# The step from cross-attention into the MLP done by token tile, and four distances of small work moved

## The chip, the cores and the metric

The kernel runs on one core of a Trainium2 chip. The metric is the device time of one execution in microseconds (us), lower is better. The engines are named as the profile names them: PE (TensorE, matrix products; PEld is its weight load), ACT (ScalarE), DVE (VectorE), POOL (GpSimd) and SP (SyncE, which here only issues the loads of weights).

## What is computed

One block of a streaming encoder, on 256 tokens of 2048 channels, everything in float32. Only the tail of the second sub-layer and the head of the third matter to most of the change:

```python
h = rms_norm(x, mix_pre_norm)
y = hybrid_mixer(h, ...)                 # gated DeltaNet, pooling, gates, output product
x = x + rms_norm(y, mix_post_norm)
h = rms_norm(x, xa_pre_norm)
m = rms_norm(mem, mem_norm)
y = memory_cross_attention(h, m, ...)    # ends with o @ w_xo, 2048 x 2048
x = x + rms_norm(y, xa_post_norm)
h = rms_norm(x, ffn_pre_norm)
u = causal_dwconv(h @ w_up, ffn_conv_w) + ffn_conv_b    # w_up: 2048 x 11008
a, b = split(u, 2)
y = (silu(a) * b) @ w_down
x = x + rms_norm(y, ffn_post_norm)
```

## The kernel before

**Weights.** Every weight product is made of three: each float32 operand is split into a rounded high part and the low rest, and high x high, high x low and low x high are added in PSUM. A weight arrives in tiles of 1 MB (`wraw`, 128 x 2048, on SP's queue). `wsplit` (L149 to L155) halves each: ACT casts 1024 columns to the high part (L153, `whi`), DVE subtracts to the low part (L154, `wlo`). Both live in rings of three buffers.

**Two kinds of product.** `proj_tm` (L190 ff.) makes 512 output channels of both token tiles (128 tokens each), tokens on the partitions: three matmuls of 512 columns for each of 16 input pieces and each token tile (L197, L198, L199). With `tail=n` its last 2n pieces are taken token tile by token tile, and `mid` is called in between; until now only the last product of the kernel (`dn3`) uses that. `proj_cm` makes one block of 128 output channels for all 256 tokens, channels on the partitions (L179): 16 matmuls with the high weights over 512 columns (high and low part of the activations side by side) and 16 with the low weights over 256.

**Small work.** The gated DeltaNet, the norms and the like are Python generators in two lanes. `tick()`, called between runs of matmuls, lets each lane take one step; `yield` or `wait(n)` in a generator is a distance of one or n ticks. So the distances decide between which matmuls small work is recorded. A scheduler then orders what is recorded, except instructions given to `pin`, which stay in program order on their engine.

**The four places of small work.** `first_convs` (L655 ff.) squares the token-major input `xt` on ACT, one 2048-wide tile after the other. `gdn_rest` makes decay matrices: two `gap` products (L734), an Exp of each on ACT (L738), a mask on POOL (L739), then four `kq` products on PE (L747) into the same ring of four PSUM tiles; further down it has a `wait(3)` after the step called p5. `mem_norm` squares the memory tokens, waits two ticks and calls `row_factors` (L294 to L311): a reduction, POOL's scale and power (L271, L273), a diagonal matrix on DVE (L305) and the matmuls `Rp` with it (L307).

**The step into the MLP** (L1182 to L1200). `pn.block` (L380 ff.) squares each product of w_xo on ACT (L279) and multiplies it by the gain on DVE (L384). `pn.scales` makes the reciprocal roots on POOL (L396, L398). For each quarter q of the channels, `pn.piece` (L401 ff., DVE L403) normalises it and adds the residual for both token tiles, `transpose_in` (L240 to L260) turns it by matmuls against `ident` (L249) into two PSUM tiles of 256 channels and splits it into the tile `h3T` (ACT L256 for the high part, DVE L258 for the low part, both reading the PSUM tile), and `square_sum` squares it (ACT L279).

**The MLP's first half.** `up(blk)` (L1203 to L1215) makes a block by `proj_cm`, adds its two halves (`cm_sum`: ACT L185, DVE L186), multiplies by the row factor (L1208) and convolves (ACT L1209, DVE L1212). Blocks come in pairs `ua`, `ub`; after `ua` follows Silu (L1219, with an activation table to load), after `ub` the product of the two and its split `gT` (L1221, ACT L238, DVE L239).

Of the kernel before, what the change touches and what calls it, by code (L numbers as in the profile page):

```python
# [8 lines left out]
F32 = mybir.dt.float32  # L9
# [16 lines left out]
def kernel(  # L26
# [102 lines left out]
    def wait(n):  # L129
        for _ in range(n):  # L130
            yield
# [26 lines left out]
    def pin(ins, keep=True):  # L158
        if keep:
            tc.keep_in_program_order(ins)  # L160
# [73 lines left out]
    def getX(tiles):  # L234
        return lambda kt: tiles[kt // 4][:, kt % 4]
# [37 lines left out]
        nc.gpsimd.tensor_tensor(out=r, in0=r, in1=mhalf[:, 0:1], op=ALU.pow)  # L273
        return r

    def square_sum(src, dst, name):

        junk = tmp.tile([P, 512], F32, tag="j512", name=f"j_{name}")
        nc.scalar.activation(junk, src, AF.Square, accum_out=dst)  # L279

    def pre_norm(src, gi, name, tiles, ss):

# [82 lines left out]
    class PostNorm:  # L365
# [11 lines left out]
                         for t in range(NT)]  # L377
            self.r = []

        def block(self, ps, nb, ts=range(NT)):  # L380
            sl = slice(nb * 512, (nb + 1) * 512)
            for t in ts:
                square_sum(ps[t], self.ss[t][:, nb:nb + 1], f"{self.name}{nb}{t}")
                nc.vector.tensor_tensor(out=self.y[t][:, sl], in0=ps[t], in1=self.g[:, sl],  # L384
                                        op=ALU.mult)
# [15 lines left out]
        def piece(self, t, q):  # L401
            sl = slice(q * 512, (q + 1) * 512)
            nc.vector.scalar_tensor_tensor(  # L403
                out=self.y[t][:, sl], in0=self.y[t][:, sl], scalar=self.r[t][:, 0:1],
                in1=self.x[t][:, sl], op0=ALU.mult, op1=ALU.add)
            return self.y[t][:, sl]


# [203 lines left out]
    def gdn_group(gi):  # L612
# [33 lines left out]
        for hl in range(4):  # L646
# [3 lines left out]
            if h == 0:  # L650
                xps = [conv_in(ps, f"{c}{n}") for c, ps in zip("qkv", ps_first)]
                dec = decays(ps_first[3])
                next(dec)

                def first_convs(n=n, hl=hl, vc=vc):  # L655
                    ss0 = [sml.tile([P, 1], F32, tag="ss", name=f"s0_{t}", bufs=4)
                           for t in range(NT)]
                    yield from wait(1)
                    for t in range(NT):
                        pin(nc.scalar.activation(xt[t], xt[t], AF.Square, accum_out=ss0[t]))  # L660
                        yield
                    yield from wait(2)
                    R0.extend(row_factors(ss0, "h", True))
                    yield
                    for i, dst in enumerate((KQ[:, hl, :, 1, :], KQ[:, hl, :, 0, :], vc)):
                        conv_silu(xps[i], i, dst, f"{'qkv'[i]}{n}", R0[0])
                        yield
                        yield
                    lanes["a"].append(head_tok(n, hl, vc))
                    yield from wait(8)  # L670

                lanes["b"].append(first_convs())
                lanes["b"].append(dec)
                z_gate(raw_z)
                continue
# [17 lines left out]
    def gdn_rest(gi, g_, KQ, V, zs, ktok, ss):  # L693
# [30 lines left out]
        for b in range(2):  # L724
# [8 lines left out]
            for a in range(2):  # L733
# [327 lines left out]
    def mem_norm():  # L1061
        mcm = [b8(f"mcm{i}").rearrange("p (k s) -> p k s", k=8) for i in range(2)]
        for i in range(2):
            nc.gpsimd.dma_start(mcm[i], mem_cm[i])
        yield from wait(8)
        ss = yield from cm_squares(mcm, "me")
        yield from wait(2)
        R, _ = row_factors(ss, "me")
        yield from wait(2)
        yield from norm_cm(mcm, R, 2, "me", memT)  # L1070
# [106 lines left out]
            step(lanes["b"])  # L1177
    A = getX(aT)
    pn = PostNorm(1, lambda t: x1[t * P:(t + 1) * P, :], "xa")
    for nb in range(4):  # L1180
        pn.block(proj_tm(w_xo[nb], A, 16, f"xo{nb}"), nb)

    x2 = dram.tile([S, D], F32, name="x2")
    pn.scales()
    ss = new_ss("h3")
    h3T = []
    for q in range(4):
        ys = [pn.piece(t, q) for t in range(NT)]  # L1190
        d = xtile(f"h3T{q}")
        transpose_in(d, lambda t: ys[t], pre_sb[:, 3, 4 * q:4 * q + 4], f"h3{q}")
        h3T.append(d)
        for t in range(NT):
            square_sum(ys[t], ss[t][:, q:q + 1], f"h3{t}{q}")
    for t in range(NT):
        nc.gpsimd.dma_start(x2[t * P:(t + 1) * P, :], pn.y[t])
    H3 = getX(h3T)
# [122 lines left out]
```

## Time and profile before

| | |
|---|---|
| three runs | 2013.08, 2013.47, 2014.16 us; median 2013.47 us |
| profiled execution | 2014.26 us, its span 2012.5 us |
| granted clock of TensorE, mean | 0.998 |
| busy, share of the span | PE 99%, PEld 85%, DVE 67%, ACT 57%, POOL 6% |
| loaded and stored | 380 MB, 188 GB/s of HBM traffic over the span |

A span is the time from the first to the last instruction of the profiled execution; 1.8 us of the execution lie outside it. The busy share of PE in the page counts modelled ends of matmuls, so 99% does not mean that a matmul of full size was always in the array. The profile's clock is given as a share of full speed: 1.00 is 2.4 GHz, 0.50 is 1.2 GHz.

### The profile page before, as it was taken

To read this page: it belongs to the slowest core of one execution; us is meant where nothing else is said; L and a number is where in the kernel's file an instruction comes from. 1 tells how busy PE (TensorE), PEld (TensorE's weight loads), DVE (VectorE), ACT (ScalarE), POOL (GpSimd) and SP (SyncE) were. 2 spreads that over 40 slices of the span, in tenths; PEclk is the share of its full clock that TensorE was granted. 3 is DMA by queue.
4 is the path that set the end of the run, shared out by engine and by line. 5 is a ranking of instruction groups with operands and counts; after the bars stand their busy time and mean duration, and the time that the engine had idled before them with its cause. 6 is when DMAs were issued, how large, how long until landed. Compare 5 with 4: busy or idle time off the path is not lost.

```text
span 2012.5 us, 27745 instructions
## 1 busy us (share of the span) xinstructions
PE 1993.8 (99%) x10842; PEld 1708.6 (85%) x10842; DVE 1346.0 (67%) x2046; ACT 1138.0 (57%) x1902; POOL 112.2 (6%) x154
## 2 busy tenths in 40 slices
PE   9999999999999999999999999999999999999998
PEld 7888888888888888888888888788888888888886
DVE  6786776768746855767555554787777777754444
ACT  6777766767655544556454444665655555544443
POOL 0420211101100000000000000100000000000000
PEclk9999999999999999999999999999999999999999
DMA  8544454444445666556555555555555555565554
GB/s 309 186 159 156 168 169 145 168 168 165 165 153 195 225 229 210 183 191 212 189 189 186 188 175 200 207 192 188 189 188 189 189 189 188 191 240 192 195 192 142
DMA packets 57333, 379.97 MB, mean 189 GB/s; under 512 B 7024, under 2 KB 8304, under 8 KB 12656
## 3 DMA queue, kind: packets, MB, share of 16 engines
q1 hardware_dynamic: 54288, 361.41, 52.6%
q0 software_dynamic: 2192, 15.73, 2.1%
q8 instruction: 85, 1.39, 0.3%
q10 hardware_dynamic: 720, 1.05, 0.2%
q14 instruction: 48, 0.39, 0.1%
HBM read 371.87 MB, written 6.29 MB: 188 GB/s over the span
## 4 chain that ended last, share of the span: by engine, by line
PE 94%; ACT 2%; DMA 2%; issue 1%; POOL 1%; DVE 1%; SPq 0%; DVEq 0%; POOLq 0%; ACTq 0%
PE cm_ua L179 12%; PE cm_ub L179 12%; PE cm_xk L179 4%; PE cm_xq L179 4%; PE cm_kg L179 4%; PE tm_dn L198 4%; PE tm_dn L197 4%; PE tm_dn L199 4%; PE cm_qg L179 4%; PE cm_vg L179 4%; PE cm_p L179 2%; PE tm_ga L198 1%; PE tm_xv L197 1%; PE tm_ya L199 1%; PE tm_xv L198 1%; PE tm_ga L199 1%
## 5 line engine op out<-in xcount | busy, mean ns | idle before, releaser
L154 DVE TENSOR_TENSOR wlo_dn<-raw_dn,whi_dn 128x1024 fp32r<-128x1024 f32 (+1 forms) x88 | 105.5, 1200 | 117.5 <-ACT whi_dn L153 117.3
L179 PE MATMUL cm_ua<-h3T,whi_ua 128*128 128x512 f32 x688 | 166.6, 393 | 0.5 <-DVE h3T L258 0.5
L153 ACT CAST whi_dn<-raw_dn 128x1024 fp32r<-128x1024 f32 (+1 forms) x88 | 91.1, 1035 | 133.1 <-PE tm_dn L199 128.4
L179 PE MATMUL cm_ub<-h3T,whi_ub 128*128 128x512 f32 x688 | 165.9, 391 | 0.0
L179 PEld LDWEIGHTS cm_ua<-h3T,whi_ua 128*128 128x128 f32 x688 | 126.6, 189 | 25.7 <-DVE h3T L258 0.9
L179 PEld LDWEIGHTS cm_ub<-h3T,whi_ub 128*128 128x128 f32 x688 | 126.6, 188 | 24.7 <-ACT whi_ub L153 0.4
L197 PE MATMUL tm_dn<-whi_dn,gT 128*128 128x512 f32 x344 | 133.8, 389 | 0.0
L198 PE MATMUL tm_dn<-wlo_dn,gT 128*128 128x512 f32 x344 | 133.8, 389 | 0.0
L199 PE MATMUL tm_dn<-whi_dn,gT 128*128 128x512 f32 x344 | 133.8, 389 | 0.0
L153 ACT CAST whi_ua<-raw_ua 128x1024 fp32r<-128x1024 f32 x86 | 90.4, 1051 | 76.3 <-PE cm_ub L179 60.5
L153 ACT CAST whi_ub<-raw_ub 128x1024 fp32r<-128x1024 f32 x86 | 90.2, 1049 | 72.2 <-PE cm_ua L179 62.2
L154 DVE TENSOR_TENSOR wlo_ua<-raw_ua,whi_ua 128x1024 fp32r<-128x1024 f32 x86 | 104.8, 1219 | 7.6 <-ACT whi_ua L153 3.0
L154 DVE TENSOR_TENSOR wlo_ub<-raw_ub,whi_ub 128x1024 fp32r<-128x1024 f32 x86 | 104.7, 1218 | 0.5 <-PE cm_ua L179 0.5
L179 PEld LDWEIGHTS cm_ua<-h3T,wlo_ua 128*128 128x128 f32 x688 | 88.3, 191 | 3.4
L179 PEld LDWEIGHTS cm_ub<-h3T,wlo_ub 128*128 128x128 f32 x688 | 88.2, 191 | 3.4
L179 PE MATMUL cm_ua<-h3T,wlo_ua 128*128 128x256 f32 x688 | 89.5, 283 | 0.0
L179 PE MATMUL cm_ub<-h3T,wlo_ub 128*128 128x256 f32 x688 | 89.2, 283 | 0.0
L1212 DVE SCALAR_TENSOR_TENSOR ua_ub<-xp,fw_sb,ua_ub 128x256 f32<-128x256 f32 x86 | 41.7, 485 | 55.2 <-ACT ua_ub L1209 53.7
L197 PEld LDWEIGHTS tm_dn<-whi_dn,gT 128*128 128x128 f32 x344 | 64.6, 188 | 13.5
L199 PEld LDWEIGHTS tm_dn<-whi_dn,gT 128*128 128x128 f32 x344 | 64.6, 188 | 13.5
L198 PEld LDWEIGHTS tm_dn<-wlo_dn,gT 128*128 128x128 f32 x344 | 64.6, 188 | 13.2
L154 DVE TENSOR_TENSOR wlo_xv<-raw_xv,whi_xv 128x1024 fp32r<-128x1024 f32 x32 | 39.1, 1225 | 40.9 <-ACT whi_xv L153 38.8
(429 smaller groups left out, 5045.5 us busy)
## 6 DMA issues: line engine op xcount, KB each, us to landing
raw_ua<-in_w_up_dram SPq DMA_DIRECT2D x43, 1024.0 KB, 4.9
raw_ub<-in_w_up_dram SPq DMA_DIRECT2D x43, 1024.0 KB, 4.9
raw_dn<-in_w_dn_dram SPq DMA_DIRECT2D x40, 1024.0 KB, 4.8
raw_gb<-in_w_gb_dram SPq DMA_DIRECT2D x16, 1024.0 KB, 4.8
raw_ga<-in_w_ga_dram SPq DMA_DIRECT2D x16, 1024.0 KB, 4.9
raw_ya<-in_w_ya_dram SPq DMA_DIRECT2D x16, 1024.0 KB, 4.9
raw_mo<-in_w_mo_dram SPq DMA_DIRECT2D x16, 1024.0 KB, 4.8
raw_xk<-in_w_xk_dram SPq DMA_DIRECT2D x16, 1024.0 KB, 4.9
```

Source lines behind the costliest of these rows:

```text
L153: pin(nc.scalar.copy(hi[:, :m], raw[:, s:s + m]), keep)
L154: pin(nc.vector.tensor_tensor(out=lo[:, :m], in0=raw[:, s:s + m], in1=hi[:, :m].bitcast(F32), op=ALU.subtract), keep)
L179: pin(nc.tensor.matmul(ps[:, 0:S] if lo else ps, lhsT=w[:, (j0 + k) * P:(j0 + k + 1) * P], rhs=xk[:, 0, :] if lo else xk.rearrange("p a s ...
L197: nc.tensor.matmul(ps[t], lhsT=xh, rhs=wh, start=(k == 0), stop=False)
L198: nc.tensor.matmul(ps[t], lhsT=xh, rhs=wl, start=False, stop=False)
L199: nc.tensor.matmul(ps[t], lhsT=xl, rhs=wh, start=False, stop=(k == KT - 1))
L1212: nc.vector.scalar_tensor_tensor(out=a, in0=xp[:, 1 + j:1 + j + S], scalar=fw_sb[:, blk, j:j + 1], in1=a, op0=ALU.mult, op1=ALU.add)
```

## The change

It has two parts. First, the step into the MLP: the last product of w_xo is taken with `tail=3`, so that token tile 0 is finished 18 matmuls ahead of token tile 1, and its norm, its scale and three of its four pieces are recorded there. The weights of the first two up blocks (`w_up[0]`, `w_up[43]`) are loaded and split ahead of that product into four tiles of their own. These two blocks are then computed by (quarter q, token tile t): `h3_in` transposes four 128 x 128 squares into one PSUM tile, `h3_split` splits them one by one (four on ACT, four on DVE), `up_mm` makes the 16 matmuls of that quarter and tile for both blocks. All this, with the pieces and squares between, is pinned in the order written. The splits of the next two blocks' weights (`up_next`) are pinned as well, three of the four halves around the last two `up_mm`, the fourth where block `ub1` is recorded. The squares of token tile 1 follow them.

Second, four distances: the squares of `first_convs` are taken in halves and its waits are set anew, `gdn_rest` yields twice in place of once after its second gap and waits 4 in place of 3 after p5, and `mem_norm` waits 4 in place of 2.

```diff
     def first_convs(n=n, hl=hl, vc=vc):
-        ss0 = [sml.tile([P, 1], F32, tag="ss", name=f"s0_{t}", bufs=4)
-               for t in range(NT)]
-        yield from wait(1)
+        ss0 = [sml.tile([P, 2], F32, tag="ss0", name=f"s0_{t}") for t in range(NT)]
         for t in range(NT):
-            pin(nc.scalar.activation(xt[t], xt[t], AF.Square, accum_out=ss0[t]))
-            yield
-        yield from wait(2)
+            for s in range(2):
+                yield
+                v = xt[t][:, 1024 * s:1024 * s + 1024]
+                pin(nc.scalar.activation(v, v, AF.Square, accum_out=ss0[t][:, s:s + 1]))
+        yield
...
-        yield from wait(8)
+        yield from wait(7)
...
-            yield
+            yield from wait(1 + b)
...
-        yield from wait(3)
+        yield from wait(4)
         subs("t5", (Me, P5, LO5, 32, Te), (P5, Me, UP5, 32, Me))
...
-        yield from wait(2)
+        yield from wait(4)
         R, _ = row_factors(ss, "me")
...
-    for nb in range(4):
+    for nb in range(3):
         pn.block(proj_tm(w_xo[nb], A, 16, f"xo{nb}"), nb)
+    up_parts = []
+    for half in range(2):
+        raw = wp.tile([P, 2048], F32, tag="raw", name=f"raw_up{half}")
+        for i in range(2):
+            hl = b8(f"wup{half}{i}", F32R)
+            sl = slice(i * 1024, (i + 1) * 1024)
+            nc.sync.dma_start(raw[:, sl], w_up[KFF * i][:, half * 1024:(half + 1) * 1024])
+            split_to(hl[:, 0:1024], hl[:, 1024:2048], raw[:, sl])
+            up_parts.append((hl[:, 0:1024], hl[:, 1024:2048]))
+    def first_token_tile(ps):
+        pn.block([ps] * 2, 3, [0])
+        pn.scales([0])
+        for q in range(3):
+            pn.piece(0, q)
+    ps = proj_tm(w_xo[3], A, 16, "xo3", 3, first_token_tile)
...
-    pn.scales()
-    h3T = []
+    h3T = [xtile(f"h3T{q}") for q in range(4)]
+    ps_up = [ps_acc(f"cm_up{i}") for i in range(2)]
+    def h3_in(q, t):
+        tp[q, t] = ps_g(f"tp_h3{q}{t}")
+        for k in range(4):
+            c = (4 * q + k) * P
+            pin(nc.tensor.transpose(tp[q, t][:, k * P:(k + 1) * P], pn.y[t][:, c:c + P], ident))
+    def h3_split(q, t):
+        tsl = slice(t * P, (t + 1) * P)
+        for k in range(4):
+            gk = pre_sb[:, 3, 4 * q + k:4 * q + k + 1]
+            v = tp[q, t][:, k * P:(k + 1) * P]
+            pin(nc.scalar.activation(h3T[q][:, k, 0, tsl], v, AF.Identity, scale=gk))
+            pin(nc.vector.scalar_tensor_tensor(out=h3T[q][:, k, 1, tsl], in0=v, scalar=gk,
+                                               in1=h3T[q][:, k, 0, tsl].bitcast(F32),
+                                               op0=ALU.mult, op1=ALU.subtract))
+    def up_mm(q, t):
+        tsl = slice(t * P, (t + 1) * P)
+        for lo in (False, True):
+            for i in range(2):
+                w = up_parts[q // 2 * 2 + i][lo]
+                for k in range(4):
+                    j = (4 * (q % 2) + k) * P
+                    kt = 4 * q + k
+                    ps = ps_up[i].rearrange("p (a s) -> p a s", a=2)
+                    out = ps[:, 0, tsl] if lo else ps[:, :, tsl]
+                    rhs = H3(kt)[:, 0, tsl] if lo else H3(kt)[:, :, tsl]
+                    pin(nc.tensor.matmul(out, lhsT=w[:, j:j + P], rhs=rhs,
+                                         start=(not lo and kt == 0), stop=(lo and kt == 15)))
...
+    h3_in(0, 0)
+    h3_in(1, 0)
+    h3_split(0, 0)
+    pn.block(ps, 3, [1], True)
+    pn.scales([1])
+    h3_split(1, 0)
+    up_mm(0, 0)
+    h3_in(2, 0)
+    pn.piece(0, 3, True)
+    h3_split(2, 0)
+    up_mm(1, 0)
+    h3_in(3, 0)
+    h3_square(0, 0)
+    pn.piece(1, 0, True)
+    pn.piece(1, 1, True)
+    h3_split(3, 0)
+    up_mm(2, 0)
+    h3_in(0, 1)
+    h3_split(0, 1)
+    h3_square(0, 1)
+    up_mm(3, 0)
+    h3_in(1, 1)
+    pn.piece(1, 2, True)
+    h3_split(1, 1)
+    h3_square(0, 2)
+    up_mm(0, 1)
+    h3_in(2, 1)
+    pn.piece(1, 3, True)
+    h3_split(2, 1)
+    h3_square(0, 3)
+    up_mm(1, 1)
+    h3_in(3, 1)
+    h3_split(3, 1)
+    up_next = [wsplit(wraw(w_up[KFF * i + 1], 2048, f"up1{i}"), 2048, f"up1{i}", True)
+               for i in range(2)]
+    first_next = [next(up_next[0])]
+    up_mm(2, 1)
+    up_mm(3, 1)
+    first_next.append(next(up_next[0]))
+    first_next.append(next(up_next[1]))
     for q in range(4):
...
+        h3_square(1, q)
...
     def up(blk, name):
-        ps = proj_cm(w_up[blk], H3, name)
+        i = blk // KFF
+        if blk % KFF > 1:
+            ps = proj_cm(w_up[blk], H3, name)
+        elif blk == 1:
+            ps = proj_cm(None, H3, name, parts=first_next[:2])
+        elif blk % KFF:
+            ps = proj_cm(None, H3, name, parts=first_next[2:] + [next(up_next[1])])
+        else:
+            ps = ps_up[i]
```

Of `gdn_rest` the two waits are shown, the first after each gap (b is 0, then 1). Now the order in which instructions stand on an engine, at three places.

**PE, behind the last product of w_xo.** `tm_xo` is that product, `tp_h` are the transposes, `cm_ua` and `cm_ub` the first two up blocks. Before, from the tenth transpose behind it on:

```order
L249 MATMUL tp_h_0_11505<-ident,py_xa_10866 128x128
L249 MATMUL tp_h_1_11514<-ident,py_xa_10866 128x128
L249 MATMUL tp_h_1_11514<-ident,py_xa_10865 128x128
L249 MATMUL tp_h_1_11514<-ident,py_xa_10866 128x128
L179 MATMUL cm_ua_11609<-h3T_11479,whi_ua_0_11612 128x512
L179 MATMUL cm_ub_11661<-h3T_11479,whi_ub_0_11664 128x512
L249 MATMUL tp_h_0_11530<-ident,py_xa_10865 128x128
L179 MATMUL cm_ua_11609<-h3T_11479,whi_ua_0_11612 128x512 x2
L249 MATMUL tp_h_1_11539<-ident,py_xa_10865 128x128
L179 MATMUL cm_ua_11609<-h3T_11479,whi_ua_0_11612 128x512
L179 MATMUL cm_ua_11609<-h3T_11504,whi_ua_0_11612 128x512
```

With the change (`cm_up` are the same two blocks; 128x2x128 is a matmul of 256 columns):

```order
L199 MATMUL tm_xo_11349<-whi_xo_14_0_11448,aT_10851 128x512
L1215 MATMUL tp_h_11506<-ident,py_xa_10871 128x128 x4
L1215 MATMUL tp_h_11511<-ident,py_xa_10871 128x128 x4
L1239 MATMUL cm_up_11504<-h3T_11500,wup_11331 128x2x128 x4
L1239 MATMUL cm_up_11505<-h3T_11500,wup_11335 128x2x128 x4
L1239 MATMUL cm_up_11504<-h3T_11500,wup_11331 128x128 x4
L1239 MATMUL cm_up_11505<-h3T_11500,wup_11335 128x128 x4
L1215 MATMUL tp_h_11554<-ident,py_xa_10871 128x128 x4
L1239 MATMUL cm_up_11504<-h3T_11501,wup_11331 128x2x128 x4
```

The matmuls of the two blocks move between the transposes, in eight groups of 16, each of half the columns, and the whole of PE's work here is in written order.

**ACT, the splits of h3** (`j_xa` and `j_h` are squares; the semaphore in brackets is what the instruction waits for, DVE_49 counts DVE's work). Before:

```order
L256 ACTIVATE h3T_11479<-tp_h_0_11480,pre_sb 128x256 [waits PE_49]
L256 ACTIVATE h3T_11479<-tp_h_1_11489,pre_sb 128x256 [waits PE_49]
L279 ACTIVATE j_h_11523,nss_h_11475<-py_xa_10865 128x512 [waits DVE_49,Activation_49]
L256 ACTIVATE h3T_11479<-tp_h_0_11480,pre_sb 128x256 [waits DVE_49]
L256 ACTIVATE h3T_11479<-tp_h_1_11489,pre_sb 128x256 [waits DVE_49]
L256 ACTIVATE h3T_11504<-tp_h_0_11505,pre_sb 128x256 [waits PE_49]
L256 ACTIVATE h3T_11504<-tp_h_1_11514,pre_sb 128x256 [waits PE_49]
```

With the change:

```order
L279 ACTIVATE j_xa_11470,pss_xa_10875<-tm_xo_11348 128x512 [waits PE_49]
L1222 ACTIVATE h3T_11500<-tp_h_11506,pre_sb 128x128 [waits PE_49]
L1222 ACTIVATE h3T_11500<-tp_h_11506,pre_sb 128x128 [waits DVE_49] x3
L279 ACTIVATE j_xa_11524,pss_xa_10876<-tm_xo_11349 128x512
L1222 ACTIVATE h3T_11501<-tp_h_11511,pre_sb 128x128 [waits PE_49]
L1222 ACTIVATE h3T_11501<-tp_h_11511,pre_sb 128x128 [waits DVE_49] x3
L1222 ACTIVATE h3T_11502<-tp_h_11554,pre_sb 128x128 [waits PE_49]
L1222 ACTIVATE h3T_11502<-tp_h_11554,pre_sb 128x128 [waits DVE_49] x3
```

Reads of two PSUM tiles in turn become four reads of one tile, the last three of them each behind a wait for DVE.

**ACT, before the last half of block `ub1`** (`t_ua` is the sum of a finished `ua` block, L1318 and L1308 are now the lines of Silu and of the first convolution step). Before, `whi_ub_1024_11774` is that half:

```order
L185 COPY t_ua_11653<-cm_ua_11609 128x256 [waits PE_49]
L153 CAST whi_ub_0_11770<-raw_ub_11768 128x1024 [waits DVE_49,DMAHW6_49,PE_49,Activation_49]
L185 COPY t_ub_11705<-cm_ub_11661 128x256 [waits PE_49]
L1209 ACTIVATE ua_ua_11652<-xp_94,fb_sb,fw_sb 128x256 [waits DVE_49]
L153 CAST whi_ub_1024_11774<-raw_ub_11768 128x1024 [waits PE_49,Activation_49]
L153 CAST whi_ua_0_11824<-raw_ua_11822 128x1024 [waits DMAHW7_49,PE_49,Activation_49]
L1219 ACT_TABLE_LOAD
L1219 ACTIVATE ua_ua_11652<-ua_ua_11652 128x256 [waits DVE_49]
L1209 ACTIVATE ua_ub_11704<-xp_96,fb_sb,fw_sb 128x256
L185 COPY t_ua_11759<-cm_ua_11715 128x256 [waits PE_49]
```

With the change it is `whi_up_1024_11875`:

```order
L185 COPY t_ua_11814<-cm_up_11504 128x256 [waits PE_49]
L185 COPY t_ub_11823<-cm_up_11505 128x256 [waits PE_49]
L1308 ACTIVATE ua_ua_11813<-xp_94,fb_sb,fw_sb 128x256 [waits DVE_49]
L1308 ACTIVATE ua_ub_11822<-xp_96,fb_sb,fw_sb 128x256 [waits DVE_49]
L185 COPY t_ua_11867<-cm_ua_11833 128x256 [waits PE_49]
L1318 ACT_TABLE_LOAD
L1318 ACTIVATE ua_ua_11813<-ua_ua_11813 128x256 [waits DVE_49]
L1308 ACTIVATE ua_ua_11866<-xp_98,fb_sb,fw_sb 128x256 [waits DVE_49]
L238 CAST gT_11802<-ua_ub_11822 128x256 [waits DVE_49]
L1318 ACTIVATE ua_ua_11866<-ua_ua_11866 128x256 [waits DVE_49]
L153 CAST whi_up_1024_11875<-raw_up_11727 128x1024
```

The cast of that half moves from before the Silu of the first pair to behind the sum, the convolution and the Silu of the second `ua` block.

## Rows read from the trace of the kernel before

**Rows 1.** The page: chain that ended last, shares of the span by engine.

```profile
PE 94%; ACT 2%; DMA 2%; issue 1%; POOL 1%; DVE 1%; SPq 0%; DVEq 0%; POOLq 0%; ACTq 0%
```

**Rows 2.** What PE waited for: us in total, times, longest.

```profile
PE kq_g L747 <- ACT UD_g L738: 3.6, 4, 0.9
PE tp_h L249 <- DVE py_xa L403: 2.5, 3, 1.3
...
PE Rp_me L307 <- DVE dg_me L305: 0.6, 1, 0.6
```

**Rows 3.** Chain that ended last, 1276 to 1316: start us, us, what.

```profile
1281.36 0.24 PE tm_xo L199
...
1283.56 2.09 DVE py_xa L403 x3
...
1290.67 0.66 PE tp_h L249 x6
...
1304.01 4.43 PE cm_ua L179 x27
1308.44 5.57 PE cm_ub L179 x32
```

**Rows 4.** Windows: length; busy PE, PEld, DVE, ACT, POOL; PEclk, DMA share, GB/s.

```profile
1282.00:1283.00 1.00, 0.08 (x1) 0.11 (x2) 0.98 (x2) 1.00 (x3) 0.51 (x2) 1.00 0.88 139
...
1287.00:1288.00 1.00, 1.00 (x6) 0.66 (x4) 1.00 (x4) 1.00 (x4) 0.00 (x0) 0.50 0.00 0
```

**Rows 5.** Timeline, 926 to 931.5: ACT and DVE on transposed tiles; brackets: idle before, releaser.

```profile
928.40 0.83 ACT L256 ACTIVATE h2T<-tp_h,pre_sb 128x256 fp32r<-128x256 f32 x2
928.90 0.88 DVE L258 SCALAR_TENSOR_TENSOR h2T<-tp_h,pre_sb,h2T 128x256 fp32r<-128x256 f32 x2 [1.44 <-ACT h2T L256]
929.42 0.86 ACT L256 ACTIVATE h2T<-tp_h,pre_sb 128x256 fp32r<-128x256 f32 x2 [0.19 <-DVE h2T L258]
```

**Rows 6.** Lines L874 and L753: shortest, median, longest ns of one 128x128 from PSUM.

```profile
L874 ACT ACTIVATE TM_g<-X_g,br_g x32: 347/362/374, 181.2 to 592.9; 128x128 f32<-128x128 f32 x32
...
L753 DVE SCALAR_TENSOR_TENSOR UD_g<-kq_g,nbr_g,UD_g x32: 340/342/351, 122.8 to 518.0; 128x128 f32<-128x128 f32 x32
```

**Rows 7.** Timeline, 1288.4: one square of 512 columns on ACT.

```profile
1288.40 0.65 ACT L279 ACTIVATE j_h<-py_xa 128x512 f32<-128x512 f32 x1
```

**Rows 8.** Chain, 81 and 836 us: matmuls of 256 columns and of one.

```profile
81.20 1.91 PE cm_kg L179 x16
...
836.00 1.69 PE sq_me L332 x16
```

**Rows 9.** Chain, 839 us: POOL's power in the row factors.

```profile
839.42 0.58 POOL rstd_me L273
```

**Rows 10.** Timeline of ACT, 1308 to 1312: after a ua block.

```profile
1308.75 1.28 ACT L1219 ACT_TABLE_LOAD   x1
1310.04 0.42 ACT L1219 ACTIVATE ua_ua<-ua_ua 128x256 f32<-128x256 f32 x1
1310.37 0.59 ACT L1209 ACTIVATE ua_ub<-xp,fb_sb,fw_sb 128x256 f32<-128x256 f32 x1
1310.86 0.35 ACT L185 COPY t_ua<-cm_ua 128x256 f32<-128x256 f32 x1
1311.11 1.05 ACT L153 CAST whi_ua<-raw_ua 128x1024 fp32r<-128x1024 f32 x1
```

**Rows 11.** Timeline, 117 to 125: kq and the Exps.

```profile
119.32 1.89 PE L747 MATMUL kq_g<-KQ_g 128*128 128x256 f32 x8
...
121.44 1.09 ACT L738 ACTIVATE UD_g<-gap_g 128x512 f32<-128x512 f32 x2
...
122.09 1.99 PE L747 MATMUL kq_g<-KQ_g 128*128 128x256 f32 x8 [0.88 <-ACT UD_g L738]
```

**Rows 12.** Timeline of ACT at the start: the first cast of w_z.

```profile
34.33 2.00 ACT L153 CAST whi_zg<-raw_z 128x1024 fp32r<-128x1024 f32 x2 [1.36 <-DMA raw_z<-in_w_z_dram]
```

**Rows 13.** Groups of ACT: the casts for w_xo, idle before them, and what ended it.

```profile
L153 ACT CAST whi_xo<-raw_xo 128x1024 fp32r<-128x1024 f32 x32 | 33.7, 1054 | 44.0 <-PE tm_xo L199 40.6 <-PE tm_xv L199 3.3
```

More of the change, by code (lines that the diff above doesn't have):

```diff
@@ L274, in rstd_of, with square_sum @@
         return r
-    def square_sum(src, dst, name):
+    def square_sum(src, dst, name, keep=False):
         junk = tmp.tile([P, 512], F32, tag="j512", name=f"j_{name}")
-        nc.scalar.activation(junk, src, AF.Square, accum_out=dst)
+        pin(nc.scalar.activation(junk, src, AF.Square, accum_out=dst), keep)
     def pre_norm(src, gi, name, tiles, ss):
@@ L378, in __init__, with block @@
             self.r = []
-        def block(self, ps, nb, ts=range(NT)):
+        def block(self, ps, nb, ts=range(NT), keep=False):
             sl = slice(nb * 512, (nb + 1) * 512)
             for t in ts:
-                square_sum(ps[t], self.ss[t][:, nb:nb + 1], f"{self.name}{nb}{t}")
-                nc.vector.tensor_tensor(out=self.y[t][:, sl], in0=ps[t], in1=self.g[:, sl],
-                                        op=ALU.mult)
+                square_sum(ps[t], self.ss[t][:, nb:nb + 1], f"{self.name}{nb}{t}", keep)
+                pin(nc.vector.tensor_tensor(out=self.y[t][:, sl], in0=ps[t],
+                                            in1=self.g[:, sl], op=ALU.mult), keep)
             if nb == 2:
@@ L399, in scales, with piece @@
                 self.r.append(r)
-        def piece(self, t, q):
+        def piece(self, t, q, keep=False):
             sl = slice(q * 512, (q + 1) * 512)
-            nc.vector.scalar_tensor_tensor(
+            pin(nc.vector.scalar_tensor_tensor(
                 out=self.y[t][:, sl], in0=self.y[t][:, sl], scalar=self.r[t][:, 0:1],
-                in1=self.x[t][:, sl], op0=ALU.mult, op1=ALU.add)
+                in1=self.x[t][:, sl], op0=ALU.mult, op1=ALU.add), keep)
             return self.y[t][:, sl]
@@ L655, in first_convs @@
                 def first_convs(n=n, hl=hl, vc=vc):
-                    ss0 = [sml.tile([P, 1], F32, tag="ss", name=f"s0_{t}", bufs=4)
-                           for t in range(NT)]
-                    yield from wait(1)
+                    ss0 = [sml.tile([P, 2], F32, tag="ss0", name=f"s0_{t}") for t in range(NT)]
                     for t in range(NT):
-                        pin(nc.scalar.activation(xt[t], xt[t], AF.Square, accum_out=ss0[t]))
-                        yield
-                    yield from wait(2)
+                        for s in range(2):
+                            yield
+                            v = xt[t][:, 1024 * s:1024 * s + 1024]
+                            pin(nc.scalar.activation(v, v, AF.Square,
+                                                     accum_out=ss0[t][:, s:s + 1]))
+                    yield
                     R0.extend(row_factors(ss0, "h", True))
@@ L1185 @@
+    def first_token_tile(ps):
[4 more added lines that the diff above has]
+    ps = proj_tm(w_xo[3], A, 16, "xo3", 3, first_token_tile)
     x2 = dram.tile([S, D], F32, name="x2")
-    pn.scales()
     ss = new_ss("h3")
-    h3T = []
-    for q in range(4):
[L1190 to L1195, printed above, removed]
+    h3T = [xtile(f"h3T{q}") for q in range(4)]
@@ new lines @@
+    H3 = getX(h3T)
+    ps_up = [ps_acc(f"cm_up{i}") for i in range(2)]
+    tp = {}
+    def h3_in(q, t):
[12 more added lines that the diff above has]
+                                               op0=ALU.mult, op1=ALU.subtract))
@@ new lines, in h3_square @@
+    def h3_square(t, q):
+        square_sum(pn.y[t][:, q * 512:(q + 1) * 512], ss[t][:, q:q + 1], f"h3{t}{q}", True)
+    h3_in(0, 0)
[17 more added lines that the diff above has]
+    h3_split(0, 1)
@@ L1196 @@
+    first_next.append(next(up_next[1]))
+    for q in range(4):
+        h3_square(1, q)
     for t in range(NT):
         nc.gpsimd.dma_start(x2[t * P:(t + 1) * P, :], pn.y[t])
-    H3 = getX(h3T)
     R3, _ = row_factors(ss, "h3")
```

## The prediction

> **What bounds the kernel now.** First the shares of the chain that ended last: PE holds 94% of it [rows 1]. Time can only go where PE waits, so the second view is what PE waited for [rows 2]: four waits for the Exp behind the `kq` products (3.6 us together), three waits of the h3 transposes for the pieces (2.5 us), one of `Rp_me` (0.6 us). The change aims at these three. The third view is the chain around the step [rows 3]: the last matmul of w_xo starts at 1281.36 and is done at 1281.60, which I call E. The third up block (`ua1`) ends at 1308.44 = E+26.84, the fourth (`ub1`) at 1308.44 + 5.57 = 1314.01 = E+32.41. The first two blocks would have ended at E+21.27 had the third run at full speed (26.84 - 5.57). The fourth view, windows of 1 us [rows 4], shows the rest of the loss: PE is busy 0.08 in the microsecond behind E, and some 4 us later the granted clock is 0.50, the lower of its two levels (1.2 GHz), in three such windows in a row, with PE always busy in the row shown. At half speed 3 us do the work of 1.5, so the dip costs up to 1.5 us, less what PE would have waited there anyway; it is part of E+32.41.
>
> **The new step, priced.** Transposes of token tile 0 can start at E at once, because three of its four pieces are done under the 18 last matmuls of tile 1 (18 x 0.23 = 4.1 us [rows 3]). That removes the three waits. What takes their place is the split.
>
> *The pair.* In the order of ACT each of the last three splits of a tile waits for DVE. The trace shows what such a wait is: ACT reads two transposed PSUM tiles from 928.40 to 929.23, and its next read, of the first of the two again, starts only at 929.42 [rows 5]. DVE's read of that tile began at 928.90. Two reads in a row overlap by about 0.1, so one of DVE's two in 0.88 us takes about 0.48 and ended at 929.38: ACT went on 0.04 us later. DVE itself began 0.03 us behind the end of ACT's first read (about 0.47 of the 0.83). Before, two tiles alternate and most of this hides. In the new order one tile is read eight times in turn: ACT 0.362, hand-over 0.03, DVE 0.342, hand-over 0.04 [rows 5, 6], 0.775 us for 128 columns. The Trainium skill says in "PSUM — Partial Sum Buffer", section "PSUM bank collisions raise a hardware error", that ACT and DVE must not access one bank (in the same partitions) at once, two reads included, so programs have to separate them by semaphores; the trace agrees, by the 0.19 us that ACT idles in the row named. By that rule four small reads of one bank cost 3.1 us where two banks in turn would cost about half, so it speaks against this layout.
>
> *A group.* A (q, t) group is four pairs. From one group's fourth ACT read to the next group's fourth: three cycles of 0.775, plus 0.26 until ACT can start the next read (0.362 less the overlap), 2.58 us with nothing between. A piece on DVE (2.09 / 3 = 0.70 [rows 3]) delays DVE's first read and brings it to 3.25, two pieces to 3.94; a square alone on ACT (0.65 [rows 7], some 0.61 of it before the next can start) makes 3.19; between the first two groups the square and gain product of w_xo's tile 1 stand, in turn on one PSUM tile, which makes 3.42. In the written order: 3.42 + 3.25 + 3.94 + 2.58 + 3.25 + 3.25 + 3.19 = 22.88 us. ACT first reads at about E+0.6 (four transposes of 0.11 [rows 3] and some 0.2 to hand over), its fourth read starts at E+2.9, the last of all at E+25.8, and DVE's last ends at E+26.5.
>
> *PE beside it.* A group is four transposes (0.44), eight matmuls of 256 columns (1.91 / 16 = 0.12 each, 0.96 [rows 8]) and eight of 128. Of the last kind no row exists. Below it is bounded by a matmul of one column, 1.69 / 16 = 0.106, above by one of 512, 0.23 [rows 3, 8]; I take 0.11, since a column count so near the lower row changes little (256 columns are at 0.12). That is 2.3 us of PE for a group against 2.6 to 3.9 of ACT and DVE: PE now waits inside every group, and even at 0.23 most of the extra lies under them. Only what follows DVE's last read counts: five matmuls of 0.12 and eight of 0.11, about 1.5 us with the wake-up. The first two blocks end at E+28.1, against E+21.27: 6.8 us late.
>
> *The row factors.* Behind the last split ACT has three casts of 1.05 (0.95 apart) and four squares (0.61 apart), to about E+31.5. The reduction, the scale, the power (0.58 [rows 9]) and the diagonal add about 1.5, E+33.0. PE has recorded the second half of `Rp` behind 14 matmuls of `ua1`, at E+28.1 + 3.2 = E+31.3: it waits 1.7. Bounds 0 and 2.5. `ua1` ends at 28.1 + 5.57 + 0.44 (four small matmuls at the transposes' 0.11) + 1.7 = E+35.8.
>
> *The fourth split.* The cast of `ub1`'s last half now stands behind the sum and convolution of `ua1` on ACT. They can only start when `ua1` is done: 0.35 (copy), 1.28 (table), 0.42, 0.59, about 0.4 (gT), 0.42, then the cast 1.05 [rows 10], 4.5 us if ACT never waited, and about 1.1 for the DVE steps between them (four of some 0.4 to 0.5, partly under the table load). PE wants it after eight matmuls of 512 columns, 1.8 us. It waits 3.7, bounds 0 (were ACT to get to it early) and 5. DVE's part of that split hides behind the other 16 matmuls. What is queued behind the cast on ACT, the next pair's, has a whole block of slack. `ub1` ends at 35.8 + 5.57 + 3.7 = E+45.1 against E+32.4: **+12.7 us**.
>
> *The clock.* The dip follows a starved PE [rows 4]. PE starts the new step with at most 0.9 us of transposes in some 2 us, so I expect one such dip again; over three microseconds a group takes PE 4.6 in place of about 3.3, once: **+0.9** (0 if no dip comes).
>
> **The distances.** *kq*: the first two tiles of `kq` run from 119.32, the third must wait for the Exp to empty a gap tile and starts at 122.09, 0.88 us idle; the two Exps run from 121.44 [rows 11]. Recorded a tick later, six matmuls of 0.23 (1.36 us) run first, more than the 0.88, and ACT's order does not move. That gives **-3.6** over the four heads' groups; bounds 0 (the wait turns up at the next user of the ring) and -4.0. *mem_norm*: two more ticks cover the 0.6 of [rows 2]: **-0.6**. *Squares at the start*: ACT's next work there waits 1.36 us for the load of w_z [rows 12], so finishing squares in other pieces brings nothing: 0. *p5*: no PE wait behind it is among the rows: 0. *Early weights*: the first pair's four casts of 1.05 and four subtractions move ahead of w_xo's last product; ACT's casts for w_xo idle 40.6 us for PE [rows 13], so they are hidden; without that cover it would be a few casts, 1 to 4 us. SP issues four smaller loads ahead of w_xo's last five, into the same ring of three raw tiles; the loads stay ahead for the same reason. POOL's scales of tile 0 move under tile 1's matmuls.
>
> **Sum.** 12.7 + 0.9 - 3.6 - 0.6 = +9.4 on the profiled 2014.26 us, which lies 0.8 above the median of the runs: 2013.47 + 9.4 = **2022.9 us**.
>
> **Rivals.** *PE sets the pace* (the other side). If ACT and DVE hand over so fast, or read side by side, that a pair costs under 0.57 us (2.3 / 4), the eight groups take 8 x 2.3 plus 1.5 before the first: E+19.9 and not E+28.1, no dip. The `Rp` wait stays about as it is. 9.4 - 8.2 - 0.9 = +0.3: 2013.8 us, no change; with the fourth split early too, 2010. For it: PE's starvation at E is gone for certain. Against it: the waits in ACT's order and the 0.04 us rows of the hand-over; the point of decision is 0.2 us below the sum of the two durations, so it needs real overlap. 12%. *The clock stays low.* If the gaps in every group keep the clock at its lower level, a group is 4.6 us of PE: 8 x 4.6 + 1.5 = E+38.3, 10.2 later, less the 0.9 already counted and the `Rp` wait of 1.7, which would be hidden: 2030.5 us. For it: 0.50 came after one starved microsecond [rows 4]. Against: groups keep PE 70% busy and the half-clock windows before ended by themselves. The Trainium skill ("TensorE: Matmul & The Clock Gate", section "A second HAM failure mode: psum-queue depth-cycling") tells of short idles between groups of matmuls that make the clock swing between its two levels. The dip of rows 4 agrees as far as one starved place can. 10%. *The distances do nothing*: their waits move to the next user of the ring: 2022.9 + 4.2 = 2027.1 us, 8%. *The fourth split is in time*: 2022.9 - 3.7 = 2019.2 us, 10%. My forecast: 60%.
>
> **Range and chances.** The forecast with its bounds (`Rp` wait gone, -1.7; small matmuls at 0.23, +1) and the third and fourth rival reach from 2017.2 to 2028. I give **2017.0 to 2029.0**; that leaves out the first rival and the low clock, about 2 in 10. A difference of 0.2%, 4.0 us, is about what a measurement of this kernel can tell from no change. Only the first rival is under +4.0: most of its 12% is no change. Faster 0.04, same 0.08, slower 0.88.
>
> **What would show it.** In the profile after: `h3_split`'s ACT reads (L1222) about 0.78 us apart with idle time ended by DVE, and PE waiting for DVE's L1223 in almost every group, 12 to 15 us in all; `up_mm` of the last group ending some 28 us behind the last w_xo matmul; one wait of `Rp_h` near 1.7 and one of `cm_ub` for ACT L153 near 3.7; the `kq` and `Rp_me` waits gone from the list. It is wrong if L1222 starts under 0.6 us apart, if `cm_ub` waits for nothing, if the clock reads 0.50 over most of the step, or if PE waits at `kq` as long as before.

## The result and the profile after

| | before | changed |
|---|---|---|
| median of four runs each | 2013.28 us | 2024.88 us |
| profiled execution, its span | 2014.26, 2012.5 us | 2024.78, 2023.1 us |
| granted clock, mean | 0.998 | 0.998 |

The ratio of the runs is 1.0059, 95% interval 1.0047 to 1.0071: the change costs 11.6 us. The profiled execution of before lies 1.0 us above its median, so between the two traces the difference is 10.6 us of span.

What PE waited for in the changed kernel (us in total, times, longest), to be laid beside [rows 2]:

```profile
PE cm_up L1239 <- DVE h3T L1223: 4.2, 12, 0.4
PE cm_ub L179 <- ACT whi_up L153: 3.5, 1, 3.5
PE Rp_h L307 <- DVE dg_h L305: 1.4, 1, 1.4
...
PE Rp_me L307 <- DVE dg_me L305: 0.4, 1, 0.4
```

The four waits at `kq` and the three for pieces are gone. Three new ones stand in their place, all behind the last w_xo product. The timeline of PE there shows the stretch (start us, us, the instruction or a run of equal ones, in brackets the idle time before and what ended it):

```profile
1277.02 0.39 PE L199 MATMUL tm_xo<-whi_xo,aT 128*128 128x512 f32 x1
1277.26 1.03 PE L1215 MATMUL tp_h<-ident,py_xa 128*128 128x128 f32 x8
1278.70 0.38 PE L1239 MATMUL cm_up<-h3T,wup 128*128 128x256 f32 x1 [0.41 <-DVE h3T L1223]
1279.48 0.38 PE L1239 MATMUL cm_up<-h3T,wup 128*128 128x256 f32 x1 [0.40 <-DVE h3T L1223]
...
1306.06 3.43 PE L179 MATMUL cm_ua<-h3T,whi_up 128*128 128x512 f32 x14
1310.86 0.49 PE L307 MATMUL Rp_h<-dg_h,ones 128*128 128x128 f32 x2 [1.37 <-DVE dg_h L305]
...
1313.57 2.03 PE L179 MATMUL cm_ub<-h3T,whi_up 128*128 128x512 f32 x8
1319.06 2.96 PE L179 MATMUL cm_ub<-h3T,whi_up 128*128 128x512 f32 x8 [3.46 <-ACT whi_up L153]
...
1324.46 1.78 PE L179 MATMUL cm_ua<-h3T,whi_ua 128*128 128x512 f32 x7
```

I read every end here as the start of what follows. The last w_xo matmul of before starts at 1281.19 and that of the changed kernel at 1277.02: **4.2 us are gained ahead of the step.** With E at the next start, 1277.26, the first two blocks end at E+28.8 (E+21.3 before at full speed of the third), `ua1` at E+36.3 (E+26.8), `ub1` at E+47.2 (E+32.4 [rows 3]): **14.8 us are lost in the step**, and 14.8 - 4.2 is the 10.6 of the spans. The loss by block: 7.5 in the first two, 1.9 in `ua1` (1.4 of them the wait), 5.3 in `ub1` (3.5 the wait).

Why the first two blocks are late is seen on ACT and DVE in the timeline of the first group:

```profile
1278.68 0.37 ACT L1222 ACTIVATE h3T<-tp_h,pre_sb 128x128 fp32r<-128x128 f32 x1 [0.42 <-DVE h3T L1223]
...
1279.08 0.35 DVE L1223 SCALAR_TENSOR_TENSOR h3T<-tp_h,pre_sb,h3T 128x128 fp32r<-128x128 f32 x1 [0.44 <-ACT h3T L1222]
1279.46 0.37 ACT L1222 ACTIVATE h3T<-tp_h,pre_sb 128x128 fp32r<-128x128 f32 x1 [0.42 <-DVE h3T L1223]
```

ACT, then DVE, then ACT, 0.78 us apart, each idle 0.42 to 0.44 us for the other while both read one PSUM tile. The two waits differ: DVE also needs the high part that ACT has just written, since it subtracts it; ACT waits only because DVE reads the same tile. PE, which has 0.12 us of work for each such pair, follows at the same distance (1278.70, 1279.48).

The rest of `ub1`'s loss is the clock. Of its windows (length; busy PE, PEld, DVE, ACT, POOL; PEclk, DMA share, GB/s) two of four in a row are:

```profile
1320.00:1321.00 1.00, 1.00 (x5) 0.76 (x4) 1.00 (x2) 0.90 (x1) 0.00 (x0) 0.53 0.00 0
...
1323.00:1324.00 1.00, 1.00 (x9) 1.00 (x9) 0.22 (x1) 0.10 (x1) 0.00 (x0) 0.77 1.00 426
```

A full clock would have done in them and in the two left out (0.50 each) 1.7 us more work. It follows the 3.5 us for which PE stood still, as the dip of [rows 4] follows the starved microsecond behind E.

### The profile page after: what moved, and what is told of

Its sections match the earlier page's. It is cut to its first block, busy times and chain, and to the rows that moved or that the text cites. A ratio compares the mean times of both kernels' runs of the same rounds, so it can differ in the third digit from the quotient of the medians.

```text
span 2023.1 us, 27890 instructions
## 1 busy us (share of the span) xinstructions
PE 2001.6 (99%) x10906; PEld 1715.6 (85%) x10906; DVE 1352.3 (67%) x2064; ACT 1146.1 (57%) x1922; POOL 111.7 (6%) x154
## 5 line engine op out<-in xcount | busy, mean ns | idle before, releaser
L179 PE MATMUL cm_ub<-h3T,whi_ub 128*128 128x512 f32 x656 | 156.5, 391 | 0.0
L179 PE MATMUL cm_ua<-h3T,whi_ua 128*128 128x512 f32 x656 | 156.5, 391 | 0.0
L179 PEld LDWEIGHTS cm_ua<-h3T,whi_ua 128*128 128x128 f32 x656 | 120.6, 188 | 23.3
L179 PEld LDWEIGHTS cm_ub<-h3T,whi_ub 128*128 128x128 f32 x656 | 120.6, 188 | 23.3
L153 ACT CAST whi_ua<-raw_ua 128x1024 fp32r<-128x1024 f32 x82 | 86.3, 1053 | 71.2 <-PE cm_ub L179 61.2
L154 DVE TENSOR_TENSOR wlo_ua<-raw_ua,whi_ua 128x1024 fp32r<-128x1024 f32 x82 | 100.0, 1220 | 6.9 <-PE cm_ub L179 2.4
L154 DVE TENSOR_TENSOR wlo_ub<-raw_ub,whi_ub 128x1024 fp32r<-128x1024 f32 x82 | 99.9, 1218 | 0.0
L179 PEld LDWEIGHTS cm_ua<-h3T,wlo_ua 128*128 128x128 f32 x656 | 84.1, 191 | 3.2
L179 PEld LDWEIGHTS cm_ub<-h3T,wlo_ub 128*128 128x128 f32 x656 | 84.1, 191 | 3.2
L179 PE MATMUL cm_ua<-h3T,wlo_ua 128*128 128x256 f32 x656 | 85.1, 283 | 0.0
```

Of the source, the lines that this page charges most:

```text
L153: pin(nc.scalar.copy(hi[:, :m], raw[:, s:s + m]), keep)
L154: pin(nc.vector.tensor_tensor(out=lo[:, :m], in0=raw[:, s:s + m], in1=hi[:, :m].bitcast(F32), op=ALU.subtract), keep)
L179: pin(nc.tensor.matmul(ps[:, 0:S] if lo else ps, lhsT=w[:, (j0 + k) * P:(j0 + k + 1) * P], rhs=xk[:, 0, :] if lo else xk.rearrange("p a s ...
```

## The experiments

Times are medians; "the distances alone" is the third run. E and the end of `ub1` are read as above.

**Two PSUM tiles in turn.** The four transposes of a group alternate between two tiles, nothing else changes:

```diff
-        tp[q, t] = ps_g(f"tp_h3{q}{t}")
+        tp[q, t] = [ps_g(f"tp_h3{q}{t}{i}") for i in range(2)]
...
-            v = tp[q, t][:, k * P:(k + 1) * P]
+            v = tp[q, t][k % 2][:, k // 2 * P:(k // 2 + 1) * P]
```

> The changed kernel, but each group's four transposes go into two PSUM tiles in turn, so that ACT and DVE alternate between tiles. Theory (the four reads of one tile in turn set the pace): the wait of up_mm for DVE in each group goes, a group falls from 3.2 us to PE's 2.3 us, the first two blocks end about 21 us behind the last w_xo matmul and not 28.8; the wait for the row factors grows to about 2.5 us since PE gets there earlier; in all 7 to 9 us less than the changed kernel, 2016 to 2018 us. Rival (the small matmuls themselves are what costs): the tiles do not matter, within 1.5 us of 2024.9 us. Rival (the clock costs it): the clock stays at 0.50 for as long as with the changed kernel and more than half of the loss remains, above 2021 us.

2017.18 us, 7.7 less. The waits for DVE in the groups are gone but for one of 0.3 us, the first two blocks end at E+20.1, and the row factors and the cast are what PE waits for:

```profile
PE cm_ub L179 <- ACT whi_up L153: 2.6, 1, 2.6
PE Rp_h L307 <- DVE dg_h L305: 2.5, 1, 2.5
...
PE cm_up L1240 <- DVE h3T L1224: 0.3, 1, 0.3
```

So the matmuls are as small and as many as before and cost 8.7 us less: it was the one tile, not their size. In ACT's timeline of this run two reads now go together (x2) and the idle time for DVE in the middle of a group, where DVE has nothing else between, is 0.16 us, not three times 0.42:

```profile
1289.06 0.63 ACT L1223 ACTIVATE h3T<-tp_h,pre_sb 128x128 fp32r<-128x128 f32 x2 [0.16 <-DVE h3T L1224]
```

The clock is at 1.00 through the first 20 us behind E and falls to 0.50 behind each of the two waits, two more examples of the order wait, then dip.

**The last half of `ub1` early.**

```diff
+    wup = b8("wup_last", F32R)
+    pin(nc.scalar.copy(wup[:, 0:1024], up_raw[1][:, 1024:2048]))
+    pin(nc.vector.tensor_tensor(out=wup[:, 1024:2048], in0=up_raw[1][:, 1024:2048],
+                                in1=wup[:, 0:1024].bitcast(F32), op=ALU.subtract))
+    first_next.append((wup[:, 0:1024], wup[:, 1024:2048]))
...
-            ps = proj_cm(None, H3, name, parts=first_next[2:] + [next(up_next[1])])
+            ps = proj_cm(None, H3, name, parts=first_next[2:])
```

> The changed kernel, but the last half of block ub1's weights is split into a tile of its own right behind the squares of token tile 1 and ahead of the small work of the first blocks. Theory: the wait of 3.5 us of cm_ub for the cast goes, and with it the clock's second dip (about 1.3 us), which is owed to that wait: 4 to 5.5 us less, 2019.5 to 2021 us. If the second dip has another cause it stays and only 3.5 us go (2021.4 us). Rival (the wait moves to the next blocks' casts): less than 1.5 us gained.

2018.93 us, 6.0 less. The 3.5 us wait is gone and so is the dip behind it; `ub1` ends at E+41.8, 5.4 earlier, which is the wait and the dip (3.5 and 1.7). The cast runs there at 1308.70, from the same load, where the changed kernel's trace has it at 1317.98: it was its place in ACT's order that it waited for. The time is 0.6 us below the range; in the trace the step also begins 0.5 us earlier than in the changed kernel's (E is 1276.73), ahead of anything that the edit touches.

The run shows one thing more. The order up to `ub1` is that of the changed kernel, but the clock stays at 1.00 in the first groups, where the changed kernel's trace has 0.50, and the first two blocks still end at E+28.8. A window of the changed kernel's trace, then the same window and the end of the first blocks (the start of the last line) in this run's:

```profile
1284.00:1285.00 1.00, 0.79 (x4) 0.50 (x4) 0.81 (x2) 0.41 (x2) 0.00 (x0) 0.50 0.00 0
...
1284.00:1285.00 1.00, 0.94 (x8) 0.94 (x9) 0.93 (x3) 0.04 (x1) 0.04 (x1) 1.00 0.00 0
...
1305.49 3.43 PE L179 MATMUL cm_ua<-h3T,whi_up 128*128 128x512 f32 x14
```

So the dip at the start of the changed kernel's step cost nothing: ACT and DVE set the pace there, and PE's slower work lay under their turns.

**The distances alone**, in the kernel before (the five edits of the diff's first half).

> The kernel before with the four distances of the change alone, the step into the MLP as before. Theory: the waits at kq go and the one at Rp_me shrinks, 3.6 to 4.5 us less than the kernel before, about 2009 us. Rival (the distances only move the waits; what lies ahead of E in the changed kernel comes from somewhere else, as the early weights): within 1.5 us of the kernel before.

2009.33 us, 3.8 less than before; ratio 0.9981, interval 0.9972 to 0.9991.

**The step alone** (the changed kernel with the distances of before).

> The changed kernel with the four distances as before. Theory: the kq waits are back (3.6 us) and the time is 3.6 to 4.5 us above the changed kernel, about 2029 us: the step alone costs some 15 us. Rival: within 1.5 us of the changed kernel, 2024.9 us.

2029.68 us, 4.8 more than the changed kernel, a little beyond the range. The `kq` waits are back, 3.6 us in four, as in [rows 2]. In its trace the step begins 1.0 us later than in that of the kernel before (E is 1282.43 against 1281.43), with longer waits near the kernel's start (PE for `cm_stq` 1.7 us in all against 0.8). In its profiled execution, at 2031.14 us the slowest of its four, the clock is at 0.50 for some 7 us in a row around the end of the first blocks, where the changed kernel's trace has it at 1.00, and `ub1` ends at E+48.4, 1.2 later than there. The two kernels have the same instructions there, so where a dip falls and how long it lasts is not fixed by the program alone.

**Both repairs together** (the two edits above).

> Two PSUM tiles in turn and the early last half together, else the changed kernel. Theory: the two add up. First two blocks about 20 us behind the last w_xo matmul (E), one wait left at the row factors of 2.5 to 2.7 us, ub1 done near E+34 to E+35, with one dip of the clock behind that wait (about 1.3 us more): 2011 to 2014 us, that is still not clearly below the kernel before, although its distances are worth 4 us. Rival (the cast that now comes earlier pushes another wait behind ub1): 2015 us or more.

2012.87 us, 12.0 less than the changed kernel: 1.7 short of the sum of the two gains, 7.7 and 6.0. Of that, 0.9 is the wait for the cast, which two tiles alone had already brought from 3.5 to 2.6 us, and 0.4 lies ahead of the step, which begins 0.3 to 0.5 us earlier in the traces of these three runs than in the changed kernel's and is counted twice in the sum. One wait is left, `Rp_h` with 2.5 us, and one dip behind it (1.7 us of work, not 1.3). `ub1` ends at E+35.9, a little later than the E+34 to E+35 expected.

**The squares early.** Both repairs, and one square of h3 behind each group in place of four behind the casts:

```diff
     h3_split(1, 0)
+    h3_square(0, 0)
...
     h3_split(3, 1)
+    h3_square(1, 2)
+    h3_square(1, 3)
...
-    for q in range(4):
-        h3_square(1, q)
```

> As the run with both edits, and the eight squares of h3 one behind each group, so that none stands behind the three casts. Theory: no wait of PE is left behind E but 0.4 us in each of the first pairs; the wait of the row factors goes and with it the dip behind it: ub1 done about E+32, against E+32.4 before and E+47 with the change: 2007.5 to 2010.5 us, at or a little below the kernel with the distances alone (2009.3 us). Rival (the row factors wait for POOL and DVE, not for the squares): the wait stays above 1.5 us and the time above 2011 us.

2009.32 us; PE waits for the row factors no longer, no dip is left, and `ub1` ends at E+32.05, in the timeline of PE:

```profile
1276.86 0.82 PE L1215 MATMUL tp_h<-ident,py_xa 128*128 128x128 f32 x6
...
1296.89 1.06 PE L307 MATMUL Rp_h<-dg_h,ones 128*128 128x128 f32 x4
...
1308.91 1.32 PE L179 MATMUL cm_ua<-h3T,whi_ua 128*128 128x512 f32 x5
```

That is the time of the distances alone, 2009.33 us, whose trace has the end of `ub1` at E+32.2: the step with these waits repaired is as good as the old step, and no better.

**The early token tile alone.** The kernel before with the distances, and the last w_xo product with `tail=3`:

```diff
+    ps = proj_tm(w_xo[3], A, 16, "xo3", 3, first_token_tile)
+    pn.block(ps, 3, [1])
...
-        ys = [pn.piece(t, q) for t in range(NT)]
+        ys = [pn.y[0][:, q * 512:(q + 1) * 512], pn.piece(1, q)]
```

> The kernel before with the four distances and the last w_xo product with tail=3 (token tile 0 and all its four pieces ahead), the rest of the step as before. Theory: finishing token tile 0 early gives nothing by itself, because each transposed PSUM tile holds both token tiles and PE's first transposes stand behind pieces of tile 1; DVE also has tile 0's pieces in the way: 1 to 4 us above the distances alone, 2010.5 to 2013.5 us. Rival (the early token tile is the good part of the step): 1.5 us or more below the distances alone, under 2007.8 us.

2010.97 us, 1.6 more than the distances alone; in the traces `ub1` ends at E+34.3 against E+32.2. PE starts four transposes of tile 0 at once and then waits longer than before in one place, since the next need tile 1, whose pieces stand behind weight splits on DVE:

```profile
1282.05 2.18 PE L249 MATMUL tp_h<-ident,py_xa 128*128 128x128 f32 x9 [4.72 <-DVE py_xa L403]
```

**One distance alone**: two ticks behind the second gap, nothing else.

```diff
-            yield
+            yield from wait(1 + b)
```

> The kernel before with one edit, two ticks in place of one behind the second gap. Theory: the four waits at kq go, and nearly the whole gain of the four distances is this one: 3 to 4 us below the kernel before, within 1 us of the distances alone (2009.3 us). Rival (the gain is spread over the four distances): less than 2 us below the kernel before.

2009.10 us, 4.1 less than before, ratio 0.9980, interval 0.9971 to 0.9989: this one line is the whole gain of the four distances, 3.8 (the 0.3 between them is within the intervals). The four `kq` products now run as one (compare [rows 11], where 0.88 us lie between two halves):

```profile
119.59 3.61 PE L747 MATMUL kq_g<-KQ_g 128*128 128x256 f32 x16
```

**Less work for PE.** The repaired step (squares early), with the low weights applied once over both token tiles:

```diff
-        for lo in (False, True):
+        for lo in (False, True)[:1 + t]:
...
-                    out = ps[:, 0, tsl] if lo else ps[:, :, tsl]
-                    rhs = H3(kt)[:, 0, tsl] if lo else H3(kt)[:, :, tsl]
+                    out = ps[:, 0, :] if lo else ps[:, :, tsl]
+                    rhs = H3(kt)[:, 0, :] if lo else H3(kt)[:, :, tsl]
```

> As the run with the squares early, but the low weights of the first two blocks are applied once over both token tiles (32 matmuls of 256 columns at 0.12 us) and not once a tile (64 of 128 at 0.12 us). Question: what is left of the step now that its waits are gone. Theory (PE's added matmuls are what keeps it from gaining): PE's work in the two blocks falls by 3.9 us, but ACT and DVE then set the pace of token tile 0's groups at about 2 us, so that only 0.5 to 1.5 us are gained: 2008 to 2009 us, and up_mm waits for DVE again, 2 to 4 us in all. If PE alone set the pace, nearly 4 us would be gained, 2005.5 us. Rival (the order ends in a wait elsewhere): no gain, 2009.3 us or more.

2008.62 us, 0.7 less. Part of that is not the edit: the kernel before, measured beside this run and the next, was at 2012.75 us, 0.4 below its median beside the others. In the traces `ub1` ends at E+31.7 against E+32.05, so the edit is worth about 0.4 us, a little under the 0.5 to 1.5 expected and too little for the times alone to show. PE's work fell by 3.3 us (64 matmuls at 0.112, as they start in the run with two tiles, against 32 at 0.12), not by 3.9; that so little of it reaches the time agrees with the theory. The waits view lists only 0.7 us at `up_mm`, where 2 to 4 was expected; by starts the two blocks end at E+19.8 and hold 15.0 us of work (32 transposes at 0.11, 96 matmuls at 0.12), so 4.8 us are lost, more than the view lists (why it can miss that stands below).

**And the groups in another order** ((0, 1) ahead of (3, 0), pieces moved to fit):

> As the run with the low weights once, with token tile 1's first group taken ahead of token tile 0's last, so that groups with much PE work and groups with little alternate, and the pieces moved to fit. Theory: half a microsecond more is gained than by the low weights alone: 2007.5 to 2008.8 us, the fastest of all these kernels. Rival: the order does not matter, within 0.3 us of the run without it.

2007.49 us, ratio to the kernel before 0.9974, interval 0.9964 to 0.9984: `ub1` ends at E+30.7, 0.9 earlier than without the new order. This version, with the distances, the two tiles, the early half, the early squares, the wide low products and the new order, is the fastest seen: 5.3 us below the kernel before as measured beside it, and so about 17 below the changed kernel.

## Why the prediction was right, and where it was off

The time lies in the range and the mechanism is the one forecast: the turns of ACT and DVE on one tile, then the fourth split. The size came out short, +9.4 us against +10.6 between the traces and +11.6 between the medians, and two parts of the sum are near by luck, as said below.

*The pair.* Forecast 0.775 us for ACT and DVE in turn on one tile; measured 0.78 to 0.79. The first run separates the cause: only the tile was changed. The Trainium skill's rule ("PSUM — Partial Sum Buffer", section "PSUM bank collisions raise a hardware error") that ACT and DVE are to be kept off one bank at a time, reads included, agrees with the 0.42 to 0.44 us for which each idles. The condition for the rival (PE sets the pace) was a pair under 0.57 us, which the pair never came near. Whether the chip would bear both reads of one tile at once was not tried: the wait stands in the program of every run here that reads one tile.

*The groups and the first blocks.* Forecast E+28.1 and 0.9 for a dip of the clock in them, E+29.0; measured E+28.8. That this is so near is luck. The dip came (0.75 to 0.50 from 1282 to 1286) and cost nothing, as the run with the early half shows; the pace of ACT and DVE alone is E+28.8, 0.7 more than the groups were priced at. The first group's fourth read starts at E+3.0 (forecast E+2.9), and from there to the last group's fourth read 23.5 us go by (forecast 22.9), 0.3 of the difference in the last group, where DVE makes a diagonal of the row factors between two splits. The matmul of 128 columns was taken at 0.11; at full clock, in the run with two tiles, such matmuls start 0.112 apart.

*The row factors.* Forecast 1.7, measured 1.4.

*The fourth split.* Forecast 3.7, measured 3.5, with the chain of steps on ACT as worked out; the second run shows it is the place in ACT's order and nothing in the weights' load.

*The clock.* This is the step that failed. From the one example of [rows 4] the prediction made a rule, "so I expect one such dip again", charged 0.9 us for it at the start of the step, and wrote down the wait of 3.7 us at `ub1` as 3.7 us. The runs showed otherwise on both counts: the dip at the start came in the changed kernel's trace and not in those of the early half and of the step alone, and was worth 0; the wait at `ub1`, itself a starved PE, was followed by a dip of 1.7 us that nothing hides. By blocks, forecast against measured: the first two 6.8 and 0.9 against 7.5, `ua1` 2.1 against 1.9, `ub1` 3.7 against 5.3, in all 13.6 against 14.8.

*The distances.* Forecast -4.2, measured -4.2 ahead of E in the changed kernel's trace, and -3.8 in the time. `kq` was undersized and the rest oversized: that one line measured -4.1 where -3.6 was forecast, and the -0.6 of `mem_norm` is not seen in the times (at `Rp_me` 0.3 to 0.4 of 0.6 us stays). The sum is right because the two misses cancel. The -4.2 is also of single traces: with the four distances E lies between 1276.4 and 1277.3, and in the two of those runs without the early weights at 1276.4 and 1276.7, so the early weights cost a few tenths of a microsecond at most, near the nothing that was forecast.

*What would show it.* One mark was wrong: "PE waiting for DVE's L1223 in almost every group, 12 to 15 us in all". It did not follow from the prediction's own sum, which leaves 28.1 - 8 x 2.3 = 9.7 us. The view lists 4.2. Between the starts of two matmuls there are 0.78 us, with 0.12 of work, but the view counts idle time from the modelled end of the first (0.38 after its start), so it shows 0.41, and shows little or nothing of shorter gaps. Measured by starts, the 28.8 us of the stretch hold 18.1 of work at full clock (eight groups of 2.26, as in the run with two tiles), so 10.7 were lost. `Rp_me` is also still on the list, with 0.4 us. Two other slips change nothing: the lower end of the bounds adds up to 2017.5, not 2017.2 (2022.9 - 1.7 - 3.7), and 0.57 lies 0.2 below the pair with its hand-overs, not below the sum of the two durations (0.70).

*The rivals.* "The distances do nothing" fell with the third run, "the fourth split is in time" with the second. "PE sets the pace" fell with the 0.78 us of the changed kernel's trace; with two tiles, in the first run, it came true: the first blocks end at E+20.1 where this rival had E+19.9. "The clock stays low" did not come about in the changed kernel's trace, but the run of the step alone shows 7 us of it in one execution, so it was a case to count.

## What to carry to other kernels

When two engines read the same product, count the PSUM tiles that they alternate over, not the reads: with one tile they took turns here, and a chain of short reads cost the sum of both engines and their hand-overs (0.78 us a pair). Cutting a product by token tile to start it earlier doubles its matmuls and its reads. Here one matmul of 512 columns (0.23 us) became two of 256 (0.12 each), which costs nearly nothing, but one of 256 (0.12) became two of 128 (0.112 each): 3.3 us more work for PE in two blocks. With the waits repaired the new step ended `ub1` at E+32.05, where the traces with the old one have E+31.6 to E+32.4; only with the low weights applied once and the groups reordered was it clearly ahead, at E+30.7. And a small distance moved by one tick, found at the top of the list of what PE waits for, was worth more than the new step.

## What the runs showed that was not expected

The six longest single waits of PE in these traces were each followed by a dip of the granted clock: the 3.5 us at `ub1` in the changed kernel and in the step alone, the 2.5 and 2.6 us in the run with two tiles, the 2.5 us in that with both repairs, the 4.7 us in that with the early token tile. In the first five the dip took 1.7 us of work on top of the wait; in the last it began before the wait was over and took more. Behind the 1.4 us of the row factors in the changed kernel the clock stays at 1.00.

The many short gaps inside the groups are less regular: the changed kernel's trace has a dip there, the runs with the early half and of the step alone, with the same order up to that place, have none, and the step alone has a long one later. The old step is no different. Behind E, PE starves there through two waits of 1.3 and 1.0 us in the kernel before, in the distances alone and in the run with one distance; the first two traces have the dip of [rows 4] and end `ub1` at E+32.4 and E+32.2, the third has none and ends it at E+31.6. What decides this stays open.
